# A decoder step on one core: weight sums held back around each output projection, known weights loaded a unit later, PSUM copies queued sooner, four down-projection groups instead of five

## The chip, the core and the metric

The kernel runs on one core of a Trainium2 chip. TensorE (PE in the profile) multiplies, VectorE (DVE), ScalarE (ACT) and GpSimd (POOL) work on what it leaves in PSUM and on SBUF, and SyncE (SP) issues the DMAs. The metric is the device time of one execution in microseconds. All data is float32; matmuls run in the fp32r format.

## What is computed

One inference step of a decoder layer: 2048 prompt positions with 16 learned positions ahead of them, and 8 samples of 8 positions each, which carry a cached past. D is 1024, the width F of the feed-forward part is 2816.

```python
def layer(x, prev_conv, prev_pool, prev_ffn, pos0, ...):
    h = rmsnorm(x, norm1_g)
    z = h @ w_in                                    # D -> 5D
    a = za * jax.nn.sigmoid(zg)
    a, new_conv = causal_dwconv(a, prev_conv, conv_dw)      # width 31
    a = jax.nn.silu(layernorm(a + conv_b, ln_g, ln_b)) @ w_conv_out
    p, new_pool = multiscale_pool(zp, prev_pool, pos0)
    p = jnp.einsum("btgc,gcd->btgd", p..., w_pool) * pool_scale
    m = jax.nn.sigmoid(gate_a) * a + jax.nn.sigmoid(gate_b) * p
    x = x + m @ w_out
    h2 = rmsnorm(x, norm2_g)
    up, new_ffn = causal_dwconv(h2 @ w_up, prev_ffn, ffn_dw)   # width 3
    v, g = up[..., :F], up[..., F:]
    x = x + (jax.nn.gelu(g) * v) @ w_down
```

A last RMS norm follows. The outputs are the normed rows and the new states of the two convolutions and the pooling.

## The kernel before

**Tiling.** Channels lie on the 128 partitions (8 chunks of D, 22 of F), positions along the free axis. The 2128 positions form three blocks of 708, 708 and 712 columns; a matmul takes half a block, 354 or 356 columns. Block 2 also holds the 64 sample columns. To keep float32 accuracy each operand is split into a rounded part `hi` and a remainder `lo`, and each product takes three matmuls (`gemm`, L328).

**Stages.** A stage runs over one block: G (the two GLU parts of `w_in`), PG (pooling and gates), C (the projection behind the convolution), WO (output projection, then the second norm), FF (feed-forward, then the last norm). The order is G, PG, C, WO, FF for block 0; PG, C, WO for block 1, then G for block 2, then FF for block 1; PG, C, WO, FF for block 2.

**Units.** A unit is the matmuls of one weight tile into one PSUM tile (48 matmuls for most). Units run in a fixed order; three can be joined and run chunk by chunk. What is done with the result (a "post") is a generator whose instructions are given out one at a time. Background work (norms, the convolution's rows, the weight sums) is a list of tasks of the same kind. The four PSUM tiles hold two banks each; 52 slots of SBUF hold everything else.

**What sets the order.** The kernel writes every engine's order itself. A planner (`Pace`) keeps a planned time per engine; after each unit, or after each product of a pair or step of a joined group, `drip` (L441) gives out steps of posts, weight splits and tasks as long as VectorE's planned time is behind TensorE's. What a matmul counts on that clock is set in `mm` (L210): 2.5 ns beside its columns. `force` finishes a task that a unit needs, `flush` the posts.

**Weights.** A weight that comes for the first time is loaded raw, split by ScalarE and VectorE, and stored to DRAM (`keep`) if it is used again. A known one is loaded already split, 1 MB for most. Loads go out on SP's queue, which works in order; `w_loads` (L274) lets them run up to `LEAD` = 4 weights ahead of the first one still in use, and there are four buffers (`wb`).

**Feed-forward in block 2.** Rows f = 0 to 2 are done as in the other blocks. From f = 3 on, `pair` (L963) makes the gate and the value of a row f from seven products of half length instead of eight, each 12 matmuls of 358 columns, 84 in all. They use sums of weight tiles (`mixed_weights`, L869, the task "mw") and of rows of h2 (`mixed_rows`, L840, "mx"). The seven products go into two PSUM tiles, x and a in one, bb and d in the other; three are copied out by ScalarE (c1, c5, c7) before the same place takes a second product. The down-projection runs in groups of f rows; between groups the running sum rests in DRAM (`xd`).

Of the kernel before, what the change touches and what calls it, by code (L numbers as in the profile page):

```python
# [52 lines left out]
PLAIN = 3  # L53
MIX_GROUPS = (2, 5, 5, 5, 5)
MIX_ROOM = 4
# [78 lines left out]
def trunk(ctx: ExitStack, tc: tile.TileContext, A, O):  # L134
# [75 lines left out]
    def mm(out, lhsT, rhs, start, stop, rate=1.0, again=False):  # L210
        nc.tensor.matmul(out, lhsT=lhsT, rhs=rhs, start=start, stop=stop, skip_group_check=again)  # L211
        pace.put("pe", size(out) * rate / 2.4 + 2.5, [out], [lhsT, rhs])

# [60 lines left out]
    def w_loads():  # L274
        while wstate["load"] < min(len(wq), wstate["first"] + LEAD):
            q = wq[wstate["load"]]
            q.known = known(q.key) is not None
            if not q.known and wstate["raws"] >= wstate["done"] + RAW_BUFS:
                break
            w_stores(wstate["load"] - W_BUFS)  # L280
            q.both = pace.alloc("wb", W_BUFS, wpool.tile([P, 2, q.n], F32R, tag="wb", name=nm("wb")))
            if q.known:
                load(q.both.bitcast(F32), known(q.key))
            else:
                q.raw = pace.alloc("raw", RAW_BUFS, wpool.tile([P, q.n], F32, tag="raw", name=nm("raw"), bufs=RAW_BUFS))
                load(q.raw, q.src)
                wstate["raws"] += 1
            wstate["load"] += 1
# [497 lines left out]
    def norm2(b, ts_):  # L786
# [6 lines left out]
        def first_mixed(c):  # L793
# [9 lines left out]
            both = S(2 * h + 4, F32R)  # L803
            two = both[:, : h + 2], both[:, h + 2 :]
            for i in range(2):
# [34 lines left out]
    def mixed_rows(b):  # L840
# [6 lines left out]
        for k in range(KC // 2):  # L847
# [11 lines left out]
            for t, (i, j) in ((ta, (1, 2)), (tb, (3, 4))):  # L859
                hi, lo = S(2 * n, F32R), S(2 * n, F32R)  # L860
                act(hi, t, AF.Copy)
                yield at(hi)
                tt(lo, t, hi.bitcast(F32), ALU.subtract)
                ops[i].append((hi[:, :n], lo[:, :n]))
                ops[j].append((hi[:, n:], lo[:, n:]))
                yield
# [96 lines left out]
    def pair(b, f):  # L963
# [9 lines left out]
        def mmf(_):  # L973
# [12 lines left out]
            def prod(o, i, c, xs, start):  # L986
                split_upto(w[i])
                wt = wq[w[i]].both
                for k, (xh, xl) in enumerate(xs):
                    a = slice(c + k * P, c + (k + 1) * P)  # L990
# [58 lines left out]
            box["c5"] = copy(pq[:, n:], a)  # L1049
            yield  # L1050
            prod(bb, 1, 0, mx[3], True)
            pu = S(2 * n)
            box["c7"] = copy(pu[:, :n], bb)
            yield
            for t in older:
                done(t)
            prod(d, 1, h, mx[2], True)
# [3 lines left out]
            yield  # L1061
            done(box["c1"])
            prod(x, 2, 0, b21, False)
            box["n"] = 5
            yield
            done(box["c7"])
            if pres[1]:
# [4 lines left out]
            yield  # L1072
            done(box["c5"])
            prod(a, 3, 0, b22, False)
# [214 lines left out]
    def w_up(m):  # L1289
        return W(("up", m), A["w_up"][m])  # L1290
# [23 lines left out]
    def FF(b, parts, last_parts):  # L1314
# [10 lines left out]
        for gs in MIX_GROUPS if b in MIXED else F_GROUPS:  # L1325
            for f in range(f0, f0 + gs):
                if b in MIXED and f >= PLAIN:
                    pair(b, f)
                else:
                    if f > 1:  # L1330
                        up(b, f, w_up(f), nd)
                    if f:
                        up(b, FC + f, w_up(FC + f), nd)
# [74 lines left out]
    def under_way():  # L1408
# [6 lines left out]
        rest = [t for t in order if not t.done and t.start <= now["i"]]  # L1415
        return posts + ws + [t for t in rest if not (quiet and t.name[0] in ("cv", "sc", "mw"))]

# [39 lines left out]
    with tc.manual_schedule():  # L1457
# [19 lines left out]
        while i < len(units):  # L1477
# [5 lines left out]
            needs = [name for u in group for name in u.needs]  # L1483
            flush(0 if group[0].wait or any(not tasks[name].done for name in needs) else 1)
            if i == 0:
# [112 lines left out]
```

## Time and profile before

| | |
|---|---|
| median of 3 runs (lowest to highest) | 3044.44 us (3044.23 to 3045.26) |
| the profiled execution | 3048.36 us, its span 3046.3 us |
| TensorE busy | 2948.9 us, 17,928 matmuls |
| VectorE, ScalarE, GpSimd busy | 2063.2, 822.0, 99.3 us |
| mean granted TensorE clock | 0.986 |
| DMA | 666.25 MB, 219 GB/s |

A row of a timeline gives the start, the length, the engine, the line, the operation with its tiles and the number of instructions, and in brackets the idle time ahead of it with what ended it. A row of a chain gives the start, the length and what the time was spent on. A row of stretches gives the length, then the busy time and the number of instructions of PE, PEld, DVE, ACT and POOL, the granted clock, the DMA share and GB/s. A row of waits gives the total, how often, and the longest.

### The profile page before, as it was taken

The page shows a single profiled execution, that of the slowest core. Times are in us where ns is not written, and L with a number is a line of the kernel's source. Part 1 is how long each engine was busy: PE and PEld are TensorE (multiplying, and loading weights), DVE is VectorE, ACT ScalarE, POOL GpSimd, SP SyncE. Part 2 cuts the span into 40 slices and gives each one's busy share as a digit, 9 for nine tenths or more (in the row PEclk, how much of TensorE's full clock was granted, in tenths as well). Part 3 has the DMA queues.
Part 4 walks back from the last instruction along what each step waited for, and adds up shares of the span by engine and source line. Part 5 has one row for each costly group of instructions (what it writes and reads, how often), then busy time and mean ns, then how long its engine had stood idle before and what let it go on. Part 6 is the DMA issues. An engine that isn't in the chain of part 4 may idle for free.

```text
span 3046.3 us, 44284 instructions
## 1 busy us (share of the span) xinstructions
PE 2948.9 (97%) x17928; PEld 2933.3 (96%) x17928; DVE 2063.2 (68%) x3030; ACT 822.0 (27%) x1248; POOL 99.3 (3%) x201
## 2 busy tenths in 40 slices
PE   7999999989999999999699999999999999999997
PEld 7999999989999999999699999999999998999997
DVE  7999988579799855642679959955764246644645
ACT  5201234232223332521320211213342122311312
POOL 0111000010000000000200000000000000000000
PEclk9999999999999999999799999999999999999998
DMA  8324564955654667776753343457977585687786
GB/s 302 135 80 165 196 217 147 341 199 192 216 201 173 216 213 253 242 284 256 272 203 135 137 152 116 168 186 260 325 251 264 185 310 205 236 295 267 240 296 219
DMA packets 192235, 666.25 MB, mean 219 GB/s; under 512 B 31264, under 2 KB 41632, under 8 KB 150176
## 3 DMA queue, kind: packets, MB, share of 16 engines
q1 hardware_dynamic: 192032, 663.43, 62.7%
q8 instruction: 141, 2.31, 0.3%
q14 instruction: 62, 0.51, 0.0%
HBM read 436.27 MB, written 227.08 MB: 218 GB/s over the span
## 4 chain that ended last, share of the span: by engine, by line
PE 88%; DVE 6%; DMA 2%; ACT 2%; issue 1%; SPq 0%; DVEq 0%; ACTq 0%
PE ps L211 88%; DVE s L182 3%; ACT s L194 2%; DVE s L178 2%; DMA s<-xd 1%; DMA wb<-keep 1%; DMA raw<-in_w_up 0%; DMA sf<-in_st_ffn 0%; DVE s L188 0%; DVE wb L178 0%; DVE rs L182 0%; SPq L203 0%; DVE rs L178 0%; DMA s<-in_x 0%; ACT wb L194 0%
## 5 line engine op out<-in xcount | busy, mean ns | idle before, releaser
L211 PE MATMUL ps<-s,wb 128*128 128x356 f32 (+2 forms) x17628 | 2909.4, 327 | 54.1 <-ACT s L194 34.3
L211 PEld LDWEIGHTS ps<-s,wb 128*128 128x128 f32 x17628 | 2890.7, 189 | 66.6 <-ACT s L194 40.0
L182 DVE SCALAR_TENSOR_TENSOR s<-s,half,s 128x708 f32<-128x708 f32 (+1 forms) x720 | 624.7, 927 | 0.3 <-ACT s L194 0.3
L194 ACT ACTIVATE s<-s 128x708 fp32r<-128x708 f32 (+9 forms) x451 | 315.3, 709 | 772.7 <-DVE s L182 392.1
L178 DVE TENSOR_TENSOR s<-s,s 128x708 fp32r<-128x708 f32 (+10 forms) x530 | 403.4, 773 | 119.7 <-ACT s L194 98.5
L178 DVE TENSOR_TENSOR s<-s,ps 128x708 f32<-128x708 f32 (+4 forms) x233 | 166.9, 725 | 313.4 <-PE ps L211 210.0
L194 ACT ACTIVATE s<-ps 128x358 f32<-128x358 f32 (+4 forms) x197 | 116.0, 601 | 620.5 <-PE ps L211 580.6
L182 DVE SCALAR_TENSOR_TENSOR s<-ps,cst,s 128x708 f32<-128x708 f32 (+3 forms) x200 | 181.7, 910 | 93.9 <-ACT s L194 89.1
L182 DVE SCALAR_TENSOR_TENSOR s<-s,cst,s 128x712 f32<-128x712 f32 (+3 forms) x188 | 156.4, 844 | 67.5 <-ACT s L194 65.9
L194 ACT ACTIVATE s<-ps,cst 128x708 f32<-128x708 f32 (+3 forms) x100 | 81.3, 815 | 428.9 <-PE ps L211 426.5
L178 DVE TENSOR_TENSOR wb<-raw,wb 128x1024 fp32r<-128x1024 f32 (+3 forms) x136 | 153.0, 1127 | 52.1 <-ACT wb L194 51.1
L194 ACT ACTIVATE wb<-raw 128x1024 fp32r<-128x1024 f32 (+3 forms) x136 | 132.2, 977 | 169.4 <-PE ps L211 125.6
L178 DVE TENSOR_TENSOR s<-raw,s 128x512 fp32r<-128x512 f32 x114 | 75.0, 686 | 87.1 <-ACT s L194 62.1
L182 DVE SCALAR_TENSOR_TENSOR s<-s,s 128x708 f32<-128x708 f32 (+2 forms) x96 | 85.4, 891 | 60.0 <-ACT s L194 58.1
L182 DVE SCALAR_TENSOR_TENSOR s<-s,ps 128x708 f32<-128x708 f32 (+5 forms) x65 | 44.0, 697 | 118.2 <-PE ps L211 108.7
L194 ACT ACTIVATE s<-raw 128x512 fp32r<-128x512 f32 x114 | 68.2, 625 | 79.3 <-DMA raw<-in_w_up 34.9
L178 DVE TENSOR_TENSOR s<-s 128x722 f32<-128x722 f32 (+6 forms) x64 | 55.3, 864 | 18.0 <-ACT s L194 16.6
L182 DVE SCALAR_TENSOR_TENSOR sc<-sa,cst,sc 128x64 f32<-128x64 f32 x232 | 46.8, 280 | 6.8 <-ACT sc L194 6.5
L199 POOL COPY s<-phist 128x15 f32<-128x15 f32 x24 | 13.1, 547 | 1067.6 <-DMA keep<-s 545.4
L194 ACT ACTIVATE s<-s,cst 128x712 f32<-128x712 f32 x38 | 33.6, 884 | 49.9 <-DVE s L178 49.9
L194 ACT ACTIVATE s<-s,half 128x708 f32<-128x708 f32 (+1 forms) x48 | 46.5, 974 | 0.8
L211 PEld LDWEIGHTS ps<-ones,s 128*128 128x128 f32 x144 | 21.3, 224 | 26.1 <-issue 25.9
(51 smaller groups left out, 367.2 us busy)
## 6 DMA issues: line engine op xcount, KB each, us to landing
wb<-keep SPq DMA_DIRECT2D x227, 1024.0 KB, 5.8
keep<-wb SPq DMA_DIRECT2D x100, 1024.0 KB, 6.3
keep<-s SPq DMA_DIRECT2D x266, 256.0 KB, 6.7
raw<-in_w_up SPq DMA_DIRECT2D x82, 512.0 KB, 5.8
wb<-keep SPq DMA_DIRECT2D x56, 640.0 KB, 4.4
raw<-in_w_in SPq DMA_DIRECT2D x40, 512.0 KB, 5.3
xd<-s SPq DMA_DIRECT2D x40, 356.0 KB, 6.7
s<-xd SPq DMA_DIRECT2D x40, 356.0 KB, 6.2
```

The source lines that it names most:

```text
L178: nc.vector.tensor_tensor(out=out, in0=a, in1=b, op=op)
L182: nc.vector.scalar_tensor_tensor(out=out, in0=a, scalar=s, in1=b, op0=op0, op1=op1)
L194: nc.scalar.activation(out, a, func, **kw)
L199: nc.gpsimd.tensor_copy(out, a)
L211: nc.tensor.matmul(out, lhsT=lhsT, rhs=rhs, start=start, stop=stop, skip_group_check=again)
```

## The change

Seven edits. The down-projection of block 2 takes its rows in four groups instead of five. A matmul counts 15.5 ns beside its columns on the planner's clock, instead of 2.5 (the small sums keep 2.5). A known weight isn't loaded as the fourth ahead, only as the third. The mixed block's h2 tiles are held by a reference, so that `room` counts their slots. In `pair` the waits for the three copies are placed earlier and that for the posts of the previous pair later. The third plain row's up-projection needs the task "mx", and that need doesn't make `flush` finish all posts. And the weight sums rest from every output projection until the second unit behind the next norm's first use, not only where a block's FF is taken in parts.

```diff
-MIX_GROUPS = (2, 5, 5, 5, 5)
+MIX_GROUPS = (6, 6, 5, 5)
...
-        pace.put("pe", size(out) * rate / 2.4 + 2.5, [out], [lhsT, rhs])
+        pace.put("pe", size(out) * rate / 2.4 + (15.5 if rate == 1.0 else 2.5), [out], [lhsT, rhs])
...
             q.known = known(q.key) is not None
+            if q.known and wstate["load"] >= wstate["first"] + LEAD - 1:
+                break
...
-            two = both[:, : h + 2], both[:, h + 2 :]
+            two = both[:, : h + 2], both[:, h + 2 :], both
...
-                ops[i].append((hi[:, :n], lo[:, :n]))
+                ops[i].append((hi[:, :n], lo[:, :n], hi, lo))
...
             box["c5"] = copy(pq[:, n:], a)
             yield
+            done(box["c1"])
             prod(bb, 1, 0, mx[3], True)
...
-            for t in older:
-                done(t)
+            done(box["c5"])
             prod(d, 1, h, mx[2], True)
...
-            done(box["c1"])
+            done(box["c7"])
             prod(x, 2, 0, b21, False)
             box["n"] = 5
             yield
-            done(box["c7"])
+            for t in older:
+                done(t)
             if pres[1]:
                 pres[1]()
             prod(bb, 2, h, mx[4], False)
...
-            done(box["c5"])
             prod(a, 3, 0, b22, False)
...
-                        up(b, f, w_up(f), nd)
+                        up(b, f, w_up(f), nd + ((("mx", b),) if b in MIXED and f == PLAIN - 1 else ()))
...
-        return posts + ws + [t for t in rest if not (quiet and t.name[0] in ("cv", "sc", "mw"))]
+        norm = any(mark["WO", b] <= now["i"] < mark.get(("G", b + 1), mark["FF", b]) + 2 for b in range(NBLK))
+        return posts + ws + [t for t in rest if not (quiet and t.name[0] in ("cv", "sc") or norm and t.name[0] == "mw")]
...
-            flush(0 if group[0].wait or any(not tasks[name].done for name in needs) else 1)
+            flush(0 if group[0].wait or any(not tasks[name].done for name in needs if name[0] != "mx") else 1)
```

**TensorE at the end of WO(1).** Before, with the last output projection's matmuls (354 columns), the small sums of two norms (`ones`, `cst`), and the first matmuls of G(2) (356 columns):

```order
L211 MATMUL ps_12890<-s_12392,wb_12681 128x354 x2
L211 MATMUL ps_12890<-s_12393,wb_12681 128x354
L211 MATMUL ps_12890<-s_12392,wb_12681 128x354
L211 MATMUL ps_12993<-ones,s_12551 128x1 x6
L211 MATMUL ps_12993<-cst,rs_13000 128x128 x6
L211 MATMUL ps_13065<-ones,s_12687 128x1 x6
L211 MATMUL ps_13065<-cst,rs_13072 128x128 x6
L211 MATMUL ps_13199<-s_13129,wb_12749 128x356
```

Of the change, where the first norm's sums now stand, between output projections 4 and 5 (counted from 0):

```order
L211 MATMUL ps_12888<-s_12622,wb_12748 128x354 x2
L211 MATMUL ps_12888<-s_12623,wb_12748 128x354
L211 MATMUL ps_12888<-s_12622,wb_12748 128x354
L211 MATMUL ps_12950<-ones,s_12805 128x1 x6
L211 MATMUL ps_12957<-s_11696,wb_12802 128x354
L211 MATMUL ps_12957<-s_11697,wb_12802 128x354
```

Its `cst` rows follow 48 matmuls later, behind projection 5. The second norm's sums have moved past G(2)'s beginning, in among its joined first units:

```order
L211 MATMUL ps_13217<-s_13159,wb_13153 128x356 x2
L211 MATMUL ps_13217<-s_13160,wb_13153 128x356
L211 MATMUL ps_13217<-s_13159,wb_13153 128x356
L211 MATMUL ps_13261<-ones,s_12751 128x1 x6
L211 MATMUL ps_13201<-s_13167,wb_13006 128x356
L211 MATMUL ps_13201<-s_13168,wb_13006 128x356
```

**VectorE in a pair.** Before, from the previous pair's remainder `lo` (the first row) on; `ps_24809` is the PSUM tile of bb and d, and the rows that follow form the gate's sum, d first and bb's second product last. In brackets is what a row waits for:

```order
L178 TENSOR_TENSOR s_24803<-s_24847,s_24802 128x712 [waits Activation_49]
L178 TENSOR_TENSOR s_24862<-s_24810,ps_24809 128x358 [waits PE_49]
L178 TENSOR_TENSOR s_24918<-s_24810,s_24862 128x358 [waits Activation_49]
L178 TENSOR_TENSOR s_24918<-s_24918,s_24862 128x358 [waits DVE_49]
L178 TENSOR_TENSOR s_24918<-s_24862,ps_24809 128x358
```

Of the change, the same five instructions; `ps_24759` is the tile of bb and d there:

```order
L178 TENSOR_TENSOR s_24804<-s_24760,ps_24759 128x358 [waits Activation_49]
L178 TENSOR_TENSOR s_24843<-s_24760,s_24804 128x358
L178 TENSOR_TENSOR s_24843<-s_24843,s_24804 128x358 [waits DVE_49]
L178 TENSOR_TENSOR s_24745<-s_24789,s_24744 128x712
L178 TENSOR_TENSOR s_24843<-s_24804,ps_24759 128x358 [waits PE_49]
```

Before, the first add waits for TensorE, and that wait covers bb's second product too, since the last add has none; now it waits for the copy c7 alone, the last add waits for the product, and `lo` stands between them. TensorE at the end of x's second product and the beginning of bb's, before and then of the change:

```order
L211 MATMUL ps_24808<-s_21726,wb_24778 128x358 x2
L211 MATMUL ps_24808<-s_21734,wb_24778 128x358 x3
L211 MATMUL ps_24808<-s_21769,wb_24778 128x358 x3
L211 MATMUL ps_24808<-s_21778,wb_24778 128x358 x3
L211 MATMUL ps_24809<-s_22111,wb_24778 128x358 [waits Activation_49]
L211 MATMUL ps_24809<-s_22112,wb_24778 128x358
```

```order
L211 MATMUL ps_24758<-s_21724,wb_24740 128x358 x2
L211 MATMUL ps_24758<-s_21732,wb_24740 128x358 x3
L211 MATMUL ps_24758<-s_21740,wb_24740 128x358 x3
L211 MATMUL ps_24758<-s_21776,wb_24740 128x358 x3
L211 MATMUL ps_24759<-s_22118,wb_24740 128x358 [waits DVE_49]
L211 MATMUL ps_24759<-s_22119,wb_24740 128x358
```

The order of the rows is the same; bb's second product waited for ScalarE's copy and now waits for VectorE's first add. ScalarE's own order inside a pair hasn't changed.

**SP at PG(1).** Before, with the load of the fourth unit's known weight (`keep_2555`) on top, two raw loads, and the eight stores of block 0's result:

```order
L203 DMA wb_9977<-keep_2555 128x2048
L203 DMA raw_10005<-in_w_up 128x1024
L203 DMA raw_10006<-in_w_up 128x1024
L207 DMA out_y<-s_4854 128x708
L207 DMA out_y<-s_4856 128x708
L207 DMA out_y<-s_4858 128x708
L207 DMA out_y<-s_4860 128x708
L207 DMA out_y<-s_4862 128x708
L207 DMA out_y<-s_4864 128x708
L207 DMA out_y<-s_4866 128x708
L207 DMA out_y<-s_4868 128x708
```

Of the change, from the last three of those stores on; the same weight is `keep_2565`:

```order
L207 DMA out_y<-s_4886 128x708
L207 DMA out_y<-s_4888 128x708
L207 DMA out_y<-s_4890 128x708
L207 DMA keep_10134<-s_10135 128x512
L207 DMA keep_10134<-s_10136 128x512
L203 DMA raw_10211<-in_w_up 128x1024
L203 DMA raw_10212<-in_w_up 128x1024
L207 DMA keep_6820<-wb_9786 256x1x768
L203 DMA wb_10234<-keep_2565 128x2048
```

The load has moved from ahead of the eight stores to behind them, two stores of a weight sum, two raw loads and the store of an earlier weight.

More of the change, by code (lines that the diff above doesn't have):

```diff
@@ L988, in prod @@
                 wt = wq[w[i]].both
-                for k, (xh, xl) in enumerate(xs):
+                for k, (xh, xl, *_) in enumerate(xs):
                     a = slice(c + k * P, c + (k + 1) * P)
```

## The prediction

> **What bounds the kernel now.** I read the page's first table, the table of waits, and then the matrix engine's clock and matmul counts in stretches.
>
> ```profile
> PE 2948.9 (97%) x17928; PEld 2933.3 (96%) x17928; DVE 2063.2 (68%) x3030; ACT 822.0 (27%) x1248; POOL 99.3 (3%) x201
> ...
> PE ps L211 <- DVE s L178: 34.5, 14, 10.5
> PE ps L211 <- ACT s L194: 34.3, 20, 5.6
> ...
> core 0: us, PE busy (x) PEld busy (x) DVE busy (x) ACT busy (x) POOL busy (x), PEclk, DMA share, GB/s
> 76.00:228.00 152.00, 152.00 (x935) 152.00 (x934) 141.88 (x162) 22.82 (x27) 16.44 (x20) 1.00 0.31 107
> 304.00:480.00 176.00, 176.00 (x1084) 175.56 (x1083) 156.08 (x193) 55.00 (x68) 8.51 (x11) 1.00 0.59 207
> 1830.00:1980.00 150.00, 150.00 (x918) 149.56 (x917) 136.95 (x166) 31.02 (x42) 0.00 (x0) 1.00 0.42 144
> 480.00:525.00 45.00, 40.41 (x241) 40.11 (x240) 35.32 (x41) 26.81 (x32) 0.00 (x0) 0.96 0.30 106
> 1480.00:1522.00 42.00, 18.71 (x88) 17.34 (x87) 30.26 (x54) 13.93 (x20) 18.29 (x32) 0.60 0.72 258
> 2552.00:2575.50 23.50, 17.51 (x102) 16.40 (x102) 9.83 (x14) 2.74 (x5) 0.00 (x0) 0.96 0.80 265
> 2575.50:2981.00 405.50, 387.98 (x2316) 383.60 (x2316) 199.73 (x337) 96.65 (x220) 0.00 (x0) 0.99 0.79 268
> ```
>
> TensorE bounds it at 97%. From 76 to 228 us it never pauses: 152 us over 935 matmuls is **162.6 ns each**, at a granted clock of 1.00. The change alters neither the number nor the shape of matmuls, so all it can win or lose is time beyond 162.6 ns apiece. The waits say that this is mostly about 69 us spent on single VectorE and ScalarE results. For each place I take its length minus its matmuls times 162.6 ns; that includes the slow clock behind a pause (0.60 in 1480 to 1522).
>
> **The change part by part.**
>
> *The norm at the end of WO(1): −31 us.* The largest hole, by TensorE's timeline:
>
> ```profile
> 1439.69 45.70 PE L211 MATMUL ps<-s,wb 128*128 128x354 f32 x280
> 1488.27 2.69 PE L211 MATMUL ps<-ones,s 128*128 128x1 f32 x12 [2.88 <-DVE s L178]
> 1493.03 2.93 PE L211 MATMUL ps<-cst,rs 128*128 128x128 f32 x12 [2.06 <-DVE rs L182]
> 1506.48 2.69 PE L211 MATMUL ps<-ones,s 128*128 128x1 f32 x12 [10.53 <-DVE s L178]
> 1511.24 2.93 PE L211 MATMUL ps<-cst,rs 128*128 128x128 f32 x12 [2.07 <-DVE rs L182]
> 1519.14 0.66 PE L211 MATMUL ps<-s,wb 128*128 128x356 f32 x1 [4.97 <-ACT s L194]
> 1520.59 39.63 PE L211 MATMUL ps<-s,wb 128*128 128x356 f32 x228 [0.79 <-DVE s L178]
> ...
> 1160.35 1.39 PE L211 MATMUL ps<-ones,s 128*128 128x1 f32 x12
> ...
> 1164.61 1.50 PE L211 MATMUL ps<-cst,rs 128*128 128x128 f32 x12
> 1165.87 19.44 PE L211 MATMUL ps<-s,wb 128*128 128x354 f32 x118
> ```
>
> Two norms run one behind the other with nothing between them. From 1439.69 to 1560.22 are 120.5 us with 280 + 1 + 228 = 509 matmuls (82.8 us) and 48 small sums, which cost 1.39 and 1.50 us per dozen where they are covered (5.8 us). The loss is 31.9 us. In the changed order the first norm's sums stand behind output projection 4 (of 0 to 7), and the second's inside G(2)'s first three units (order shown above): the weight sums rest, so VectorE reaches the norm's squares earlier. The six `cst` sums of the first norm then have 96 matmuls (15.6 us) between them and G(2), and eight chunks are taken up over 144 matmuls. What is late next is the second norm's `ones`: 24 VectorE instructions lie between the first norm's result and it, some 20 us at 0.82 each (as the adds in the next fence), against 150 matmuls, 24 us. It fits, so −31, bounds −33 and −24. The weight sums themselves aren't dropped; they are issued elsewhere, see the packing below.
>
> *The start of C(0): −5.5 us.* The window 480 to 525 holds 241 matmuls, 39.2 us, in 45: 5.8 lost. The chain there:
>
> ```profile
> 487.35 0.74 ACT s L194
> 488.09 0.95 ACT wb L194
> ...
> 489.07 1.22 DVE wb L178
> 490.29 0.81 DVE s L182
> 491.10 0.82 DVE s L178
> ...
> 491.96 3.17 PE ps L211 x10
> ```
>
> A weight's split and the conv norm's first chunk run in series, 4.6 us. With a matmul counted at 163.0 instead of 150.0 ns (354 columns: 147.5 + 15.5), the planner queues 8.7% more VectorE work per matmul, and the first two chunks now stand a unit earlier. Bounds −6 and −3.
>
> *One down-projection group less: −6.5 us.* In 2552 to 2575.5 stand 102 matmuls, 16.6 us: 6.9 lost. Two f rows make units of 12 matmuls (2 us), while each needs its running sum from DRAM, and the chain of waits goes through those fetches:
>
> ```profile
> 2563.36 4.91 DMA s<-xd
> ...
> 2569.66 7.13 DMA s<-xd
> ```
>
> The eight units, adds, loads of the sum, stores and weights go (8 VectorE adds and 24 DMAs in all); their matmuls move into groups of six, whose units last 36 × 162.6 ns = 5.9 us. Bounds −7 and −5.
>
> *The pairs: −14 us.* 2575.5 to 2981 holds 19 pairs of 84 matmuls at 358 columns (162.6 × 358/354 = 164.4 ns, 262.4 us) and 720 others (117.1 us): 379.5 of 405.5 us, 26 lost. One pair's ScalarE, VectorE and TensorE timeline:
>
> ```profile
> L211 PE MATMUL ps<-s,wb 128*128 128x358 f32 (+1 forms) x2316 | 388.6, 329 | 21.2 <-ACT s L194 17.5 <-DMA wb<-keep 3.6
> ...
> 2619.26 0.80 ACT L194 ACTIVATE s<-s 128x712 fp32r<-128x712 f32 x1 [3.36 <-DVE s L178]
> 2619.96 0.81 ACT L194 ACTIVATE s<-ps 128x358 f32<-128x358 f32 x2
> 2622.74 0.53 DVE L178 TENSOR_TENSOR s<-s,ps 128x358 f32<-128x358 f32 x1 [1.75 <-PE ps L211]
> 2623.18 1.09 DVE L178 TENSOR_TENSOR s<-s,s 128x358 f32<-128x358 f32 x2
> 2624.19 0.52 DVE L178 TENSOR_TENSOR s<-s,ps 128x358 f32<-128x358 f32 x1
> 2620.46 14.12 PE L211 MATMUL ps<-s,wb 128*128 128x358 f32 x84 [1.49 <-ACT s L194]
> 2635.73 1.58 PE L211 MATMUL ps<-s,wb 128*128 128x358 f32 x8 [1.15 <-ACT s L194]
> ```
>
> TensorE stops ahead of a pair's sixth product until ScalarE has copied the third out of the same PSUM buffer, and that copy is queued behind the previous pair's rounding (2619.26). One turn of this ring takes 2635.73 − 2620.46 = 15.27 us against 84 × 164.4 ns = 13.81. In the changed program ScalarE's order in a pair is **the same**, so the copy comes no sooner in its queue. What changes is that the first add no longer waits for the sixth product (it stood idle 1.75 us for it): three adds leave the ring, 2624.19 − 2622.74 = 1.45 us. In exchange TensorE now waits for that first add, 0.53 us and a hand-over of some 0.05. The turn becomes 15.27 − 1.45 + 0.58 = 14.40; of each 1.46 lost, 0.87 goes. Of 17.5 us idle owed to ScalarE some 60 to 70% goes, 10.5 to 12; the 3.6 of DMA ahead of the first pair goes with the small group, though pair 3 then comes 16 us sooner after the norm, with the mixed rows' sums just queued. Bounds −21 (the new wait is hidden) and −7.
>
> *Known weights a unit later: +4 at PG(1), +5 elsewhere.* A load's own waits are the same; it only stands further back in SP's in-order queue. In front of PG(1)'s fourth unit it falls behind the eight stores of the final norm:
>
> ```profile
> 1156.25 0.32 SPq L203 DMA_DIRECT2D wb<-keep  x1
> ...
> 1167.93 6.66 SPq L207 DMA_DIRECT2D out_y<-s  x8
> ...
> wb<-keep SPq DMA_DIRECT2D x4, 1024.0 KB, 7.1
> ```
>
> Before, it went out at 1156.25. Now it follows the stores, which end at 1174.6, two stores of a weight sum, two raw loads and a store: about 1177, and it lands 7.1 later, 1184. By the order its unit starts 90 matmuls after 1165.87, at 1180.5: a stall of 3.5 us, say 4 with the clock; 0 if those issues cost little, 10 if the queued 1.8 MB goes first. Five more loads come near their unit (the fourth units of G(2) and PG(2), output projections 3 and 4 of WO(2), the last down-projection group): 1 us each, bounds 0 and 12 together.
>
> *Packing: +2 us.* VectorE's shares above are 93, 89 and 91%; times 1.087 that is 101, 96 and 99%. At 1.4% over, 404 us of such stretches make it 6 us late, which the four PSUM buffers (up to three units of 48 × 162.6 ns = 7.8 us) should cover. Bounds 0 and 8. Fewer waits in WO(1) for the weight sums are paid here, beside matmuls.
>
> **Sum:** −31 − 5.5 − 6.5 − 14 + 4 + 5 + 2 = **−46 us**. The profiled execution took 3048.4 us (its span 3046.3), 4 above the median, so 3002 there and 3044.4 − 46 = 2998 for a median.
>
> **Where the Trainium skill bears on it.** The clock after a pause: the window 1480 to 1522 was granted 0.60 and 480 to 525 0.96, while the pair stretch, with pauses of 1.1 to 1.5 us, kept 0.99. The Trainium skill (TensorE: Matmul & The Clock Gate, section What's actually happening) says that an idle window of about 3.4 us drops the clock to half and a busy one brings it back. These rows agree; by it a PG(1) stall just above that length would cost an estimated 1.7 us more and one below it nothing, which would put the sum at −44 or leave it.
>
> **Rivals.**
> 1. *The pairs keep their pauses*, because PSUM buffers are what lacks and not the place in a queue. For it: ScalarE's order is unchanged, and the waiting product writes a buffer that is still being read. Against: 1.45 us leaves the ring. It gives 2998 + 14 = 3012. The Trainium skill (Perfetto Trace Analysis, section Optimization Strategy) reads a gap that repeats on the busy engine as a possible lack of buffers; by it this case holds, the trace bears it out only in part.
> 2. *The pairs lose all pauses*: the copy and the add fit beside the fifth product. 2998 − 8 = 2990.
> 3. *Late weights at more places.* Each fetch that falls behind a row of stores costs 7.1 us less what lead is left; at four more joins of 5 us, 2998 + 20 = 3018.
> 4. *VectorE becomes the bound* (slower). Place: the three packed stretches of the table, 478 us. The planner now counts matmuls at their real pace, so whatever takes longer than it plans adds up. It decides from a demand of 1.19: 478 × 0.19 = 91 us, less three covers of 15 (two units), takes up the 46. At 1.30 it would be 2998 + 143 − 45 = 3096. Against: 1.01 is the highest that the rows give.
>
> **How the numbers follow.** The forecast has 0.60, rival 1 0.12, rival 2 0.12, rival 3 0.11, rival 4 0.05. The parts' bounds add up to −67 and −9; all at once on one end is unlikely, so the range goes from 2981 (rival 2 with no late weights) to 3019 (rival 3). That leaves out rival 4 and some of the tails. About 0.2% is what a measurement of this kernel can tell from no change. Rivals 1 to 3 all stay faster than 3038: faster 0.94, same 0.02, slower 0.04 (most of rival 4).
>
> **What would show it.** No TensorE pause above 3 us between output projection 7 and G(2), and `ones` sums a dozen at a time amid other matmuls. Pauses ahead of a pair's sixth product of about half a microsecond, released by VectorE and no longer by ScalarE. One new pause by a weight load ahead of PG(1)'s fourth unit. The stretch 76 to 480 still without pauses. I am wrong if pairs still take 15.3 us, if the second norm's sums still hold TensorE in G(2), or if waits for weights grow beyond 20 us in all.

## The result, and the profile after

The changed kernel takes **3013.84 us** (median of 4 runs, 3012.95 to 3017.43) against 3044.85 for the kernel before on the same chip: a ratio of 0.9899, 95% interval [0.9882, 0.9916], 31 us less. The forecast was 46 less, in a range from 63 to 25 less. The profiled execution took 3014.54 us, its span 3012.8.

The first table of the page after, and its clock and matmul counts in stretches (columns as before: length, busy time and count of PE, PEld, DVE, ACT and POOL, granted clock, DMA share, GB/s):

```profile
PE 2936.2 (97%) x17928; PEld 2923.5 (97%) x17928; DVE 2046.5 (68%) x3022; ACT 821.6 (27%) x1248; POOL 106.5 (4%) x201
```

```profile
76.00:228.00 152.00, 152.00 (x938) 152.00 (x938) 150.88 (x174) 24.97 (x30) 19.22 (x20) 1.00 0.33 118
304.00:480.00 176.00, 176.00 (x1084) 175.56 (x1083) 165.45 (x205) 59.63 (x74) 10.97 (x11) 1.00 0.59 206
480.00:525.00 45.00, 45.00 (x279) 45.00 (x278) 34.44 (x39) 25.14 (x31) 0.00 (x0) 1.00 0.38 135
1480.00:1522.00 42.00, 42.00 (x268) 42.00 (x267) 32.53 (x49) 15.43 (x20) 9.65 (x19) 1.00 0.42 159
```

The two windows that held the large losses, 480 to 525 and 1480 to 1522, are full now (279 matmuls for 241, 268 for 88). A window at a fixed time holds other matmuls after the change than before. But outside block 2's feed-forward, where the down-projection's groups changed, nearly all large matmuls keep their order, so the loss of a place can be compared over the same matmuls in both traces: its length less 162.6 ns for each matmul. (Small sums count as matmuls here, so a place without pauses can come out a little below zero.)

| place | loss before, us | after | difference | forecast |
|---|---|---|---|---|
| end of WO(1) to G(2) | 29.8 | −2.4 | −32.2 | −31 |
| start of C(0) | 6.2 | 0.1 | −6.1 | −5.5 |
| first output projection of WO(0) | 0.4 | 2.0 | +1.7 | none |
| the small down-projection group | 9.5 | 1.7 | −7.8 | −6.5 |
| the 19 pairs (length less 13.81 each) | 26.2 | 20.4 | −5.8 | −14 |
| PG(1), fourth unit | −0.6 | 8.4 | +9.0 | +4 |
| start of FF(2) | 2.1 | 6.3 | +4.3 | part of +5 |
| last down-projection group | 12.2 | 14.7 | +2.5 | part of +5 |
| first units; start of FF(0) | 25.1 | 25.1 | 0 | none |
| packing | | | 0 | +2 |

The differences add up to −34.4; the two profiled executions are 33.8 us apart. (The small group's place holds a first pair, so 1 to 2 us of it stand in two rows.) Against the forecast's −46 that lacks 11.6: 8 in the pairs, 5 at PG(1), while the other rows nearly cancel. (The medians lie 31 apart, since the profiled execution of before took 3.5 us more than its median and that of after 0.7 more.)

**The norms at WO(1)'s end** now stand amid other matmuls, by TensorE's timeline (start, length, operation, count):

```profile
1465.78 1.39 PE L211 MATMUL ps<-ones,s 128*128 128x1 f32 x12
1467.04 8.06 PE L211 MATMUL ps<-s,wb 128*128 128x354 f32 x48
1474.94 1.50 PE L211 MATMUL ps<-cst,rs 128*128 128x128 f32 x12
1476.19 24.63 PE L211 MATMUL ps<-s,wb 128*128 128x354 f32 x150
1500.66 1.39 PE L211 MATMUL ps<-ones,s 128*128 128x1 f32 x12
```

No row has a bracket: nothing waits.

**The fourth unit of PG(1)** does wait. TensorE's timeline, SyncE's, and the answer for the tile `wb` over the three DMAs issued from 1172 to 1176 us (a store of a weight, this load at 1174.06 and the next one; the middle value is this load's):

```profile
1161.06 14.91 PE L211 MATMUL ps<-s,wb 128*128 128x354 f32 x90
1183.10 17.13 PE L211 MATMUL ps<-s,wb 128*128 128x354 f32 x94 [7.13 <-ACT s L194]
```

```profile
1163.12 6.45 SPq L207 DMA_DIRECT2D out_y<-s  x8
1169.66 1.61 SPq L207 DMA_DIRECT2D keep<-s  x2
1171.32 1.48 SPq L203 DMA_DIRECT2D raw<-in_w_up  x2
1172.85 0.52 SPq L207 DMA_DIRECT2D keep<-wb  x1
1174.06 6.78 SPq L203 DMA_DIRECT2D wb<-keep  x4
```

```profile
DMA to landing us min/median/max: 7.6/8.9/9.2
```

The bracket names ScalarE, but the load is issued at 1174.06 and 8.9 us later is 1183.0, 0.1 before TensorE goes on. The runs below that move the load agree: without its lateness the pause is gone.

**A pair after the change**, one turn by the timeline of TensorE, ScalarE and VectorE:

```profile
2661.17 14.10 PE L211 MATMUL ps<-s,wb 128*128 128x358 f32 x84 [1.08 <-DVE s L178]
...
2669.38 0.47 ACT L194 ACTIVATE s<-ps 128x358 f32<-128x358 f32 x1 [0.66 <-PE ps L211]
2669.75 0.88 ACT L194 ACTIVATE s<-s,cst 128x712 f32<-128x712 f32 x1
...
2670.66 1.96 DVE L182 SCALAR_TENSOR_TENSOR s<-s,cst,s 128x712 f32<-128x712 f32 x2 [2.33 <-ACT s L194]
...
2673.65 0.90 DVE L178 TENSOR_TENSOR s<-s,s 128x712 f32<-128x712 f32 x1
2674.58 0.80 ACT L194 ACTIVATE s<-s 128x712 fp32r<-128x712 f32 x1 [3.35 <-DVE s L178]
2675.28 0.81 ACT L194 ACTIVATE s<-ps 128x358 f32<-128x358 f32 x2
2675.77 0.53 DVE L178 TENSOR_TENSOR s<-s,ps 128x358 f32<-128x358 f32 x1 [1.22 <-ACT s L194]
...
2676.35 14.10 PE L211 MATMUL ps<-s,wb 128*128 128x358 f32 x84 [1.08 <-DVE s L178]
```

A turn takes 15.18 us. The pause stands where the forecast put it, ahead of the sixth product, and VectorE's first add releases it, as forecast; but it is 1.08 us and not half a microsecond. The row that matters is 2669.38: ScalarE's first copy out of PSUM waits for TensorE. From the pause's end to it are four products (the sixth, the seventh, and the next pair's x and a): 48 × 164.4 ns = 7.9 us, and about 0.3 for the last matmul to end. From the copy to the next pause's end are 6.97 us: the convolution's first step queued right behind the copy, VectorE's rows, the rounding, the last copies, the add. 8.21 + 6.97 = 15.18: that is the ring now. The copy c1 reads product x, done 2 us earlier; but in the program's order it stands behind product a, which goes to the other half of the same PSUM tile, and it waits for both.

### The profile page after: what moved, and what is told of

Same layout as the page of the kernel before. It is cut to its first block, busy times and chain, and to the rows that moved or that the text cites. A ratio compares the mean times of both kernels' runs of the same rounds, so it can differ in the third digit from the quotient of the medians.

```text
span 3012.8 us, 44237 instructions
## 1 busy us (share of the span) xinstructions
PE 2936.2 (97%) x17928; PEld 2923.5 (97%) x17928; DVE 2046.5 (68%) x3022; ACT 821.6 (27%) x1248; POOL 106.5 (4%) x201
## 4 chain that ended last, share of the span: by engine, by line
PE 90%; DVE 6%; ACT 2%; DMA 2%; issue 1%; SPq 0%; DVEq 0%; ACTq 0%
PE ps L211 90%; DVE s L182 3%; ACT s L194 2%; DVE s L178 1%; DMA wb<-keep 1%; DVE wb L178 0%; DMA raw<-in_w_in 0%; ACT wb L194 0%; SPq L203 0%; DVE s L188 0%; DVE rs L182 0%; DVE rs L178 0%; DMA s<-in_x 0%; DVE rs L190 0%; SPq L207 0%
## 5 line engine op out<-in xcount | busy, mean ns | idle before, releaser
L194 ACT ACTIVATE s<-s 128x708 f32<-128x708 f32 (+8 forms) x451 | 317.1, 710 | 858.7 <-DVE s L182 458.9
L178 DVE TENSOR_TENSOR s<-s,ps 128x708 f32<-128x708 f32 (+4 forms) x225 | 159.8, 719 | 314.7 <-PE ps L211 243.4
L199 POOL CAST s<-hhist 128x2 fp32r<-128x2 f32 x48 | 16.7, 374 | 611.2 <-PE ps L211 392.6
```

The lines of the kernel that those rows point to most:

```text
L178: nc.vector.tensor_tensor(out=out, in0=a, in1=b, op=op)
L194: nc.scalar.activation(out, a, func, **kw)
L199: nc.gpsimd.tensor_copy(out, a)
```

## The experiments

Ratios are against the kernel before on the same chip, with 95% intervals; 0.9899 is the changed kernel's. Seven runs are one edit of the changed kernel each; "those two together" and the last two are two edits. The runs were made on more than one chip, and in their series the kernel before took 3044.85 to 3046.69 us, so a difference of 2 us between two medians says nothing.

| run | median us | ratio |
|---|---|---|
| sums don't rest | 3028.95 | 0.9946 [0.9931, 0.9961] |
| products in another order | 2995.52 | 0.9835 [0.9819, 0.9852] |
| loads late only round a norm | 3007.25 | 0.9875 [0.9860, 0.9889] |
| those two together | 2993.28 | 0.9827 [0.9812, 0.9841] |
| loads as before | 3022.11 | 0.9923 [0.9907, 0.9940] |
| pair as before | 3022.04 | 0.9921 [0.9906, 0.9935] |
| planner's pace as before | 3030.91 | 0.9951 [0.9937, 0.9966] |
| five groups | 3027.64 | 0.9939 [0.9924, 0.9954] |
| resting and pace undone | 3042.24 | 0.9985 [0.9975, 0.9994] |
| other order, loads early at two places | 2989.03 | 0.9811 [0.9797, 0.9826] |

### The pair's products in another order

```diff
             box["c1"] = copy(pq[:, :n], x)
             yield
-            prod(a, 0, h, mx[1], True)
-            w_start(w[1])
-            box["c5"] = copy(pq[:, n:], a)
-            yield
-            done(box["c1"])
             prod(bb, 1, 0, mx[3], True)
             pu = S(2 * n)
             box["c7"] = copy(pu[:, :n], bb)
             yield
+            done(box["c1"])
+            prod(a, 0, h, mx[1], True)
+            w_start(w[1])
+            done(box["c7"])
+            box["c5"] = copy(pq[:, n:], a)
             done(box["c5"])
+            yield
             prod(d, 1, h, mx[2], True)
...
-            done(box["c7"])
             prod(x, 2, 0, b21, False)
```

> The pair's products are issued in another order (the second product of the other chain goes ahead of the second product of this one), so that each PSUM copy of ScalarE waits only for its own product and is not queued behind one that comes later. Nothing else changes. My theory: the pause of 1.07 us that every pair still has comes from ScalarE's first copy, which waits for the product that shares its PSUM tile while the next value conversion stands behind it in ScalarE's queue; with this order the turn of a pair falls from 15.17 to 13.8 to 14.1 us, the loss in the pairs from 20 to 0 to 6 us, and the time is 2994 to 3002. Rival: PSUM buffers are what lacks, whatever the order; the pause only changes its place, the turn stays at 15.0 to 15.3 and the time at 3011 to 3018.

2995.52 us, 18 less than the changed kernel. The stretch of the pairs in this run, and ScalarE beside TensorE in one pair:

```profile
2546.00:2926.00 380.00, 380.00 (x2316) 378.55 (x2315) 192.72 (x329) 96.84 (x213) 0.00 (x0) 1.00 0.77 272
```

```profile
2639.77 32.50 PE L211 MATMUL ps<-s,wb 128*128 128x358 f32 x196
...
2650.92 0.45 ACT L194 ACTIVATE s<-ps 128x358 f32<-128x358 f32 x1
2651.27 0.88 ACT L194 ACTIVATE s<-s,cst 128x712 f32<-128x712 f32 x1
```

TensorE doesn't pause once in 380 us, and the copy ahead of the convolution's step has no bracket: it waits for nothing. The turn is 13.8 to 13.9 us (15.32 in the first pair alone); the 19 pairs take 264.9 us for 282.8. No buffer was added, so PSUM buffers were not what lacked: the order of the products made one copy wait for a product that it doesn't read, with the rest of ScalarE's queue behind it.

### The pair as before the change

```diff
-            done(box["c1"])
             prod(bb, 1, 0, mx[3], True)
...
-            done(box["c5"])
+            for t in older:
+                done(t)
             prod(d, 1, h, mx[2], True)
...
-            done(box["c7"])
+            done(box["c1"])
             prod(x, 2, 0, b21, False)
...
-            for t in older:
-                done(t)
+            done(box["c7"])
...
+            done(box["c5"])
             prod(a, 3, 0, b22, False)
```

> The order of copies and adds within a pair as before the change, all else as in the changed kernel. My theory: the ring of a pair runs through ScalarE's first copy, which waits for a product of TensorE, and on to VectorE's first add; the old order puts one split of 0.9 us on VectorE ahead of that add, so the turn goes from 15.17 to 15.4 to 15.7 us, 14 turns cost 3 to 8 us, and the time is 3017 to 3022. Rival: the order within the pair does nothing, and the 0.1 us that the turn won came from the planner's pace; the turn stays at 15.1 to 15.3 and the time at 3012 to 3016.

3022.04 us, 8 more; the turn is 15.58 to 15.69. VectorE and TensorE in this run's timeline:

```profile
2662.97 0.90 DVE L178 TENSOR_TENSOR s<-s,s 128x712 fp32r<-128x712 f32 x1 [0.86 <-ACT s L194]
2663.79 0.52 DVE L178 TENSOR_TENSOR s<-s,ps 128x358 f32<-128x358 f32 x1
...
2664.36 14.05 PE L211 MATMUL ps<-s,wb 128*128 128x358 f32 x84 [1.53 <-DVE s L178]
```

The split of 0.90 us stands ahead of the first add, as expected, and makes the pause 1.53 us long. The turn is the expected one, the time at the edge of what was expected. So the edit of the pair is worth 0.45 us a turn beside the other edits. But the old order is slower here (15.6) than it was in the kernel before (15.27): there the first add stood behind the sixth product, and here ahead of it. Some other edit made that move, and the pair's edit more than made up for it; which one wasn't tried.

### The sums don't rest

```diff
-        norm = any(mark["WO", b] <= now["i"] < mark.get(("G", b + 1), mark["FF", b]) + 2 for b in range(NBLK))
-        return posts + ws + [t for t in rest if not (quiet and t.name[0] in ("cv", "sc") or norm and t.name[0] == "mw")]
+        return posts + ws + [t for t in rest if not (quiet and t.name[0] in ("cv", "sc", "mw"))]
```

> Weight sums are queued around the output projection again (the one line on resting undone), all else as in the changed kernel. My theory: the stretch from WO(1) to G(2) wins its 31 us by the resting alone; without it the two norms follow one another again, the loss there is 25 to 32 us, and the time is 3039 to 3046. Rival: the planner's real matmul pace would have brought the sums forward by itself; then the loss there is below 8 us and the time 3014 to 3020.

3028.95 us, 15 more: between the two. The loss at the end of WO(1) is 12.6 us, not 29.8. TensorE's timeline there:

```profile
1493.39 1.62 PE L211 MATMUL ps<-cst,rs 128*128 128x128 f32 x12 [2.06 <-DVE rs L182]
1495.29 2.69 PE L211 MATMUL ps<-ones,s 128*128 128x1 f32 x12 [0.28 <-DVE s L178]
1500.05 2.93 PE L211 MATMUL ps<-cst,rs 128*128 128x128 f32 x12 [2.07 <-DVE rs L182]
1507.26 0.66 PE L211 MATMUL ps<-s,wb 128*128 128x356 f32 x1 [4.28 <-ACT s L194]
```

The two norms stand one behind the other as before the change, but the second `ones` waits 0.28 us instead of 10.53: VectorE now takes the second norm's squares ahead of the eight chunks that the first norm scales. So the order on TensorE alone doesn't make that loss; what VectorE has queued between the two does.

### The planner's pace as before, and both undone

```diff
-        pace.put("pe", size(out) * rate / 2.4 + (15.5 if rate == 1.0 else 2.5), [out], [lhsT, rhs])
+        pace.put("pe", size(out) * rate / 2.4 + 2.5, [out], [lhsT, rhs])
```

> The planner counts a matmul at the old, shorter time, all else as in the changed kernel. My theory: the pace brings the conv norm's first chunks ahead of C(0) and nothing at WO(1)'s end, where the norm sums stand within a dozen matmuls of where the changed kernel has them; C(0)'s start loses its 6 us again, and the time is 3017 to 3022. Rival: the pace brings the half of the 31 us at WO(1)'s end that the resting was shown not to bring; that stretch loses 12 to 16 us, and the time is 3028 to 3036.

3030.91 us, 17 more, the rival's number, and not its place: the end of WO(1) loses nothing (−2.4, as in the changed kernel). C(0)'s start loses its 6.4 us again, as the theory said. The rest stands where neither looked, at PG(2)'s fourth unit. SyncE and TensorE there:

```profile
2162.17 6.40 SPq L207 DMA_DIRECT2D out_y<-s  x8
2168.66 5.80 SPq L207 DMA_DIRECT2D keep<-s  x8
2174.51 1.32 SPq L203 DMA_DIRECT2D raw<-in_w_up  x2
2175.93 1.45 SPq L203 DMA_DIRECT2D wb<-keep  x3
...
2183.60 6.60 PE L211 MATMUL ps<-s,wb 128*128 128x356 f32 x23 [9.95 <-DMA wb<-keep]
```

The late load falls behind sixteen stores, and the place loses 12.0 us more than in the changed kernel. In the changed kernel the norm's sums stand behind the same number of matmuls, but no weight sums are stored there: the load goes out directly behind the eight `out_y` stores, at 2161.0 us, and the pause is 0.38. So what this run loses here comes from the stores and raw loads ahead of the load.

Then both edits undone, resting and pace:

> The weight sums are queued around the output projections again and the planner counts a matmul at the old, shorter time; all else as in the changed kernel. With the resting alone undone the stretch around the end of WO(1) was seen to lose half of the 31 us that it lost before the change, with the pace alone undone nothing. My theory: either edit is enough for a part, because both only decide how much VectorE has in its queue ahead of the second norm's squares; with both undone the whole loss is back, 25 to 32 us there and 6 at C(0)'s start, and the time is 3048 to 3060. Rival: the other half was won by the late loads of known weights and not by the pace; the stretch loses 12 to 16 us as with the resting alone undone, and the time is 3034 to 3044.

3042.24 us, the rival's time. The end of WO(1) loses 22.3 us, between the theory and its rival, and both missed it; there the second `ones` waits for nothing, and the largest pause, 9.56 us, stands ahead of G(2)'s first matmul, for ScalarE. Over the same matmuls the kernels give: before 29.8, both undone 22.3, resting undone 12.6, loads undone (next) 8.8, pace undone −2.4, the changed kernel −2.4. Undoing no single edit brings the 32 us back, and undoing the pace brings some back only where the sums don't rest either: three edits take part. How the last 7.5 us, from 22.3 to 29.8, divide among the late loads and the others is open. PG(2)'s fourth unit loses no more here than in the changed kernel, although pace and loads are the same as in the run before; so the 12 us there take the old pace, the late loads and the resting together.

### Known weights loaded as before

```diff
-            if q.known and wstate["load"] >= wstate["first"] + LEAD - 1:
-                break
```

> Known weights are loaded as early as before the change at every place; the sums still rest around the output projections, all else as in the changed kernel. In the program's order the first norm's last sums and the second norm's then stand directly ahead of G(2) again. My theory: the late loads cost 7.8 us at PG(1)'s fourth unit and 3 at the last down-projection group, which come back here, but they are part of what keeps the two norms at WO(1)'s end apart; 12 to 22 us are lost there again, and the time is 3014 to 3025. Rival: the resting alone sets that stretch; it stays below 5 us lost, and the time is 3003 to 3008.

3022.11 us, as the theory said. Its profiled execution, at 3016.37, is the fastest of its four runs, only 1.8 us above the changed kernel's; where the other three lose 6 us more is in no trace. In the profiled one PG(1)'s pause is gone (−0.6 instead of 8.4), the last group loses 11.0 instead of 14.7, and the end of WO(1) loses 8.8, 11.2 more than in the changed kernel (the theory said 12 to 22). A second norm, in FF(1), lost 5 us with early loads, which nobody had expected. The late loads thus help to place the norms, and PG(1) is their price.

### Loads late only round a norm, alone and with the other order

```diff
-            if q.known and wstate["load"] >= wstate["first"] + LEAD - 1:
+            late = any(mark["WO", b] + -1 <= now["i"] < mark.get(("G", b + 1), mark["FF", b]) + 2 for b in range(NBLK))
+            if q.known and late and wstate["load"] >= wstate["first"] + LEAD - 1:
                 break
```

> Known weights are loaded a unit later only from one unit ahead of an output projection to two units behind the norm; elsewhere as early as before the change. My theory: late loads cost 7.8 us at PG(1)'s fourth unit and some 7 us at the last down-projection group, and are not needed there; without them, with the sums at rest as in the changed kernel, the time is 2998 to 3002, the WO(1) stretch stays without loss, and no pause by a weight load is left ahead of PG(1)'s fourth unit. Rival: the queue of stores holds up whatever load comes near it, so that an earlier place in the queue delays other loads or the sums instead; the time is 3010 to 3016 with the pause at another place.

3007.25 us: 6.6 of the 12 to 16 expected. TensorE at PG(1), and then in FF(1):

```profile
1159.97 30.20 PE L211 MATMUL ps<-s,wb 128*128 128x354 f32 x184
```

```profile
1872.41 1.47 PE L211 MATMUL ps<-ones,s 128*128 128x1 f32 x12 [1.95 <-DVE s L178]
1873.74 6.67 PE L211 MATMUL ps<-s,wb 128*128 128x354 f32 x30
```

PG(1)'s pause is gone, and with it 9 us, which shows that the load made it and not ScalarE. But FF(1) and PG(2) lose 3.8 and 3.1 us more over the same matmuls; the last group gives 3.2. The norm sums stand behind the same matmuls there as in the changed kernel. In FF(1) they wait 1.95 us for VectorE; why VectorE comes later there than in the changed kernel stays open. In PG(2) the norm doesn't wait: the pause, 2.07 us, stands ahead of a later unit and ends at 2170.63. The weight load that this unit waits for went out at 2163.71, behind eight `out_y` stores and ten stores of weight sums, and landed 6.8 us later, at 2170.50. The profile names ScalarE, whose copy ended in the same 0.1 us, so either may have held the unit to the end. The rival's number was nearer; its mechanism, a load that comes late behind stores at another place, fits PG(2); for FF(1) it isn't shown.

> Both at once: known weights late only around an output projection and its norm, and the pair's products in the other order. My theory: the two gains lie at different places and add up, 15 + 15 us off the changed kernel's 3014, so 2979 to 2987. Rival: the pairs that run faster meet the weight loads and running sums of their own groups, and 5 to 10 us of it come back as waits for loads: 2988 to 2996.

2993.28 us: the rival's number again. But the pairs keep their turn (13.8 to 14.3 behind the first) and give back 0.8 us, so its mechanism isn't what is seen; FF(1) and PG(2) lose 4.0 and 3.1 us as in the run before, and the last group gives no more than there.

### The other order, with early loads at two places only

```diff
-            if q.known and wstate["load"] >= wstate["first"] + LEAD - 1:
+            early = mark["PG", 1] - 1 <= now["i"] < mark["PG", 1] + 3 or now["i"] >= len(units) - 20
+            if q.known and not early and wstate["load"] >= wstate["first"] + LEAD - 1:
                 break
```

> The pair's products in the other order, and known weights late everywhere as in the changed kernel but for two places, PG(1)'s fourth unit and the last down-projection group, where they are loaded as early as before the change. The norm sums stand on TensorE where the changed kernel has them. My theory: the two late places cost 9 and 3 us, and the losses that came up with early loads elsewhere (4 each in FF(1) and PG(2)) came from other places of the norm sums, which stay put here; so 12 us less than the 2995.5 of the order alone, 2981 to 2987. Rival: an earlier load only moves what stands behind it in SP's queue, and the losses come up again within the same two stretches; 2990 to 2996.

2989.03 us (2988.05 to 2992.12): 6.5 less than the order alone, between the two expectations, and the fastest of all, 25 us below the changed kernel and 0.9811 of the one before. TensorE at PG(1):

```profile
1161.41 28.85 PE L211 MATMUL ps<-s,wb 128*128 128x354 f32 x175
```

PG(1) loses 8.9 us less than with the order alone and the last group 2.0 less, near what was said (9 and 3); a pause of 2.19 us for a weight load before a down projection of FF(1) (at 2105 us) and 1.5 us more at WO(0) came up in exchange. FF(1)'s norm and PG(2) lose nothing beside the order alone, as expected, but not for the reason given: in FF(1) and PG(2) the norm sums stand behind the same matmuls in the runs with early loads, too.

### Five groups

```diff
-MIX_GROUPS = (6, 6, 5, 5)
+MIX_GROUPS = (2, 5, 5, 5, 5)
```

> The mixed rows' down projection in five groups, the first of two f rows, as before the change; all else as in the changed kernel. My theory: the small group's short units wait for their running sums again, 5 to 8 us, and the time is 3019 to 3022. Rival: with the planner's pace and the late loads its loads are queued otherwise and are hidden, or FF(2)'s first units, which lost 4 us after the change, get them back; the time is 3010 to 3016.

3027.64 us, 14 more, where 5 to 8 were expected. TensorE in the small group:

```profile
2543.62 5.68 PE L211 MATMUL ps<-s,wb 128*128 128x356 f32 x24 [3.50 <-DMA wb<-keep]
2550.57 2.17 PE L211 MATMUL ps<-s,wb 128*128 128x356 f32 x12 [1.26 <-DMA wb<-keep]
2555.80 4.16 PE L211 MATMUL ps<-s,wb 128*128 128x358 f32 x24 [3.06 <-DMA wb<-keep]
```

Units of 2 us wait for weights that are loaded a unit later, and not, by these rows, for their running sums: the loss over the group is 12.6 us, 9.5 in the kernel before, 1.7 in the changed one. With late loads the small group is dearer than it was, so taking it away is worth more.

## Why the prediction was right and where it failed

The gains and losses came at the places that were forecast, but for the start of FF(2). The result lies 16 us above the forecast; by the two traces the pairs make 8 of it and PG(1) 5.

- **The end of WO(1), −31: right in place and size** (−32.2). As to the cause it was too simple. "The weight sums rest, so VectorE reaches the norm's squares earlier" is one of three edits that act there; without it 15 of the 32 come back, not all.
- **C(0), −5.5: right** (−6.1), and the planner's pace is the cause: with the old pace the loss was back. It gave 1.7 back at WO(0)'s first projection, which had no term.
- **The small group, −6.5: right** (−7.8), and 11 beside the late loads by the run that puts it back. Of the reason given, the fetch of the running sums, that run shows nothing: its waits name the weights. In the kernel before, too, 4.4 of TensorE's 6.0 us of waits there name weights, 3.6 of them ahead of the first pair, which the forecast counted with the pairs.
- **The pairs, −14: mis-sized, and here the prediction failed.** −5.8 came, and most of that in the first two pairs, where waits for loads went with the small group (16.21 and 17.54 us became 13.84 and 15.19). The steady turn went only from 15.27 to 15.17. The step "the turn becomes 15.27 − 1.45 + 0.58 = 14.40" took the ring that bound the pairs and shortened it, without asking for the next one. It stood in the timeline of before, in two rows of ScalarE further down:

```profile
2628.65 0.80 ACT L194 ACTIVATE s<-s 128x712 f32<-128x712 f32 x1 [2.77 <-DVE s L182]
2629.35 0.45 ACT L194 ACTIVATE s<-ps 128x358 f32<-128x358 f32 x1
```

  The sixth product began at 2620.46, so product a of the next pair ended 8.21 us later, at 2628.67; the copy began at 2629.35, directly behind the row ahead of it. The wait for TensorE thus lay 0.7 us under the one that was seen, and took over as soon as ScalarE's queue ran that much earlier. The rows of before would have given the turn: four products and the last matmul's end, some 8.2, then 6.38 from the copy (2629.35) to the next pause's end (2635.73), and 0.58 for the new wait are some 15.2. Nor was it the pair's edit alone that took the adds out of the ring: with the pair as before, the first add still stands ahead of the sixth product.
- **Rival 1, pairs keep their pauses, 3012:** its number is nearest to the result (3013.8), and its reason, too few PSUM buffers, was wrong. The section Optimization Strategy of Perfetto Trace Analysis, in the Trainium skill, reads such a repeated gap as a possible lack of buffers; the other order of the products took every pause away with the same buffers.
- **PG(1), +4: right in place and mechanism, mis-sized at 9.0.** The load landed at 1183.0 where 1184 was forecast, and that is luck: by the forecast's own sum everything ahead moved up by 5 us, the stores (done at 1169.57 for 1174.6) as well as TensorE (there at 1175.97 for 1180.5), which alone would leave the stall as it was. Mis-sized were the way from the last store to the load, 4.5 us for 2.4, and the landing, 8.9 for 7.1; together they make the stall 7.1 us for 3.5. The slow clock behind it cost another 1.7, as the forecast estimated.
- **Other late loads, +5: about right in sum** (+6.8, bounds 0 and 12), but of the five places that were named the last group paid 2.5, PG(2) a pause of 0.38, and the other three nothing that shows. The rest came at the start of FF(2): 6.3 us are lost there, 3.3 with loads as before and 2.7 with the old pace, so it is not the loads alone; one pause there, of 1.69 us, waits for a weight, another, of 1.97, for VectorE.
- **Packing, +2: nothing.** VectorE is busy 150.88 of 152 us in the stretch 76 to 228 and 165.45 of 176 in the next, 99 and 94% where the forecast worked out 101 and 96, and TensorE doesn't pause in either.
- What would have shown it wrong: pairs still at 15.3 us. They are at 15.2, and that sign was right to be there.

## What to carry to other kernels

When a wait in a ring goes, look for the second-longest wait in the same turn before its gain is counted: how long each instruction of the ring had been ready when it started is in the timeline. An instruction in an in-order queue should wait for the data that it reads and for nothing written to the same tile later; reordering the producers cost nothing here and won 18 us. Edits to an order that a planner makes can't be priced one by one: here three acted on the end of WO(1), the late loads cost 12 us at PG(2) where the sums rested and the pace was the old one, and with them the small group lost 12.6 us instead of 9.5.

## What the runs showed of the hardware

**The clock can fall after pauses of 2 us.** TensorE's granted clock in stretches of 3 to 5 us right behind a pause: in the changed kernel behind pauses of 1.97 us (FF(2)), 7.13 us (PG(1)) and 1.56 us (last group); in the run with late loads only round a norm behind the 1.95 us in FF(1):

```profile
2492.60:2496.00 3.40, 3.00 (x11) 2.74 (x12) 2.23 (x5) 1.45 (x3) 0.00 (x0) 0.71 0.02 5
2496.00:2500.00 4.00, 4.00 (x22) 4.00 (x22) 3.93 (x9) 1.08 (x2) 0.00 (x0) 0.82 0.00 0
...
1183.10:1187.00 3.90, 3.90 (x14) 3.90 (x15) 2.96 (x4) 1.78 (x3) 1.03 (x2) 0.53 1.00 423
...
2948.25:2953.00 4.75, 4.75 (x29) 4.75 (x30) 3.30 (x7) 1.80 (x4) 0.00 (x0) 1.00 0.36 101
```

```profile
1872.40:1876.00 3.60, 3.59 (x20) 3.60 (x21) 3.13 (x12) 0.49 (x1) 0.00 (x0) 0.72 0.61 255
1876.00:1880.00 4.00, 4.00 (x22) 4.00 (x22) 0.00 (x0) 0.00 (x0) 0.00 (x0) 0.83 0.00 0
```

Behind 1.95 and 1.97 us the clock was 0.72 and 0.71 for some 3.5 us and 0.82 or 0.83 for 4 more; behind 1.56 us it stayed at 1.00, and so it did behind the pairs' 1.08. The Trainium skill (TensorE: Matmul & The Clock Gate, What's actually happening) puts the idle window at about 3.4 us; here two pauses a little over half as long were enough, so that such a pause cost nearly twice its length: the 30 matmuls in the row at 1873.74 took 6.67 us, 1.8 more than 30 × 162.6 ns. The length alone doesn't decide it: the clock also stayed at 1.00 behind the 2.19 us in FF(1) of the run with early loads at two places, and behind the 3.06 us in the run with five groups. What decides between 2 and 3 us, these runs don't show.

**The profile names one releaser of several.** PG(1)'s pause was put down to ScalarE; taking the load forward removed it in four runs. A landing 0.1 us before the pause's end was the better witness there, as at PG(2) in the run with late loads only round a norm, where the load and the named copy end together.
